# A Mamba-2 scan without a state between its two chunks, and five weight units whose low halves are made by ScalarE and a DMA

## The chip, the cores and the metric

The kernel runs on one core of a Trainium2 chip. The metric is device time in microseconds (us), the median of several executions. TensorE (PE) multiplies, VectorE (DVE), ScalarE (ACT) and GpSimd (POOL) do elementwise work, SyncE (SP) issues the loads of the weights, and POOL issues the other DMAs. Each engine runs its instructions in the order written, and waits on semaphores for the others.

## The reference

Two decoder layers over 256 tokens of width 1024, all in float32. Each layer is a half SwiGLU, a mixer and a half SwiGLU, each followed by a layer norm. The mixer of the first layer is sparse attention; the mixer of the second, which matters here, is a Mamba-2 scan in two chunks of 128 tokens, 32 heads of 64 in 4 groups, state size 128:

```python
cb = jnp.einsum('bclgn,bcsgn->bcgls', cm, bm)
y_diag = jnp.einsum('bcgrls,bcsgrp->bclgrp', cb[:, :, :, None] * decay, xdt)
decay_to_end = jnp.exp(a_cs_l[:, :, -1:] - a_cs_l)
states = jnp.einsum('bclgn,bclgrp->bcgrpn', bm, xdt * decay_to_end[..., None])
...
y_off = jnp.einsum('bclgn,bcgrpn->bclgrp', cm, prev) * jnp.exp(a_cs_l)[..., None]
return (y_diag + y_off).reshape(bsz, seq, n_h, p_dim)
```

The state is zero before the first chunk, so `prev` of the second chunk is `states` of the first, and `y_off` matters for the second chunk alone.

## The kernel before

**Weights.** All weights are streamed from HBM as 512 KB tiles `raw` (128 partitions by 1024). A "unit" is one such tile, split for TensorE into a high half `wh` (ACT, rounded to fp32r, line 327; line 325 where a scale is folded in) and a low half `wl` = raw - wh (DVE, lines 352 and 349). Each product is three matmuls: high by high, high by low, low by high (`mm3`, lines 530 to 532). The class `Weights` plans this: `make` emits a high half and puts the unit on the list `late`, `lows` emits the low halves of that list, `prefetch` (called there) issues the next loads on SP, `pump` calls these as units are used up. At most 10 split units exist (`SLOTS`); in the scan layer 4 raw tiles are in flight (`W.raws = 4`). In the SwiGLU layers some sums of weight tiles are made by accumulating DMAs from POOL's queue (`add`, line 267). Raw tiles share the 12 buffers "f4" with other 128x1024 tiles.

**The scan layer** (`ssd`) has 58 units, called u to u+57 here. Its order is written out by hand: units 0 to 9 for the gate z and dt, 10 to 17 for B and C (`bc_tile`), 18 to 21 for x of group 0, and then for each group g a list `f` of eight pieces of projection work, between which the steps of the scan are put. In groups 0 and 1 these are the x tiles of the next group (units 22 to 25 and 30 to 33, banks `pxs`) and the z columns (26 to 29 and 34 to 37); in group 2 the last x tiles (38, 40, 42, 44) and the first units of the output matrix (39, 41, ...), which alone carry a scale (line 325). Units are split some ten units ahead of their use. For group g the scan does, in this order:

```python
f[0](); x_tok(0, g); x_tok(1, g); x_end(g); f[1](); f[2]()
py[0] = diag(0, g); state(g); gate(0, g, py[0]); decay_load(0, g + 1); f[3]()
carry(g); square(0); root(0); py[1] = diag(1, g); gate(1, g, py[1]); decay_load(1, g + 1); f[4](); ...
```

`diag` is 8 products in plain float32 (two passes each, so 16 matmuls, L1534), into one of the two PSUM banks `ptr`; `gate` (DVE, L1551 and L1552) reads that bank; `decay_load` is a DMA on POOL's queue (L1436, tile `M`, an f4 buffer). `state` multiplies B with x (L1540) and copies the result to SBUF (ACT, L1542); `carry` multiplies C with that (L1546) and adds it to chunk 1 (DVE, L1547 and L1548). B in token order (`btok`) comes from four transposes (`b_tr`, L1470, and ACT's copy L1471), beside the products of C and B of each chunk (`cb`, L1477).

Of the kernel before, what the change touches and what calls it, by code (L numbers as in the profile page):

```python
# [10 lines left out]
F32 = mybir.dt.float32  # L11
F32R = mybir.dt.float32r
AF = mybir.ActivationFunctionType
ALU = mybir.AluOpType
# [10 lines left out]
KVR = 256  # L25
# [7 lines left out]
RMS_EPS = 1e-6  # L33
# [8 lines left out]
class Plan:  # L42
# [5 lines left out]
    def __init__(self):  # L48
        self.raws, self.forms = [], []
# [159 lines left out]
class Weights:  # L209

    def __init__(self, nc, raw_tile, split_pool, src, widths, forms, slots, raws):
        self.nc, self.raw_tile, self.sp, self.src = nc, raw_tile, split_pool, src
        self.widths, self.forms, self.slots, self.raws = widths, forms, slots, raws
        self.offs = np.concatenate([[0], np.cumsum(np.array(widths) * 128)]).tolist()
        self.n, self.nraw = len(forms), len(widths)
        self.loaded = self.summed = self.made = self.done = self.dead = self.debt = 0
        self.defer = False  # L220
        self.scale = {}
        self.raw, self.hl, self.late = {}, {}, []
        self.uses = {}
        self.added, self.prior = set(), {}
        self.adds = [u for u, f in enumerate(forms) if f[2]]
        last = {}
        for u, f in enumerate(forms):
            self.prior[u] = last.get(f[0], (-1, None))
            last[f[0]] = (u, u)
            if f[1] is not None:  # L230
                last[f[1]] = (last.get(f[1], (-1, None))[0], u)
            for r in f[:2]:
                if r is not None:
                    self.uses[r] = self.uses.get(r, 0) + 1
# [75 lines left out]
    def make(self, between=None):  # L310

        nc, u = self.nc, self.made
        r = self.forms[u][0]
        if self.summed <= u:
            self.sum()
        raw = self.raw[r]
        w = self.widths[r]  # L320
        h = self.sp.tile([128, 1024], F32R, name=f"wh{u}", tag="wh", bufs=self.slots)
        lo = self.sp.tile([128, 1024], F32R, name=f"wl{u}", tag="wl", bufs=self.slots)
        for c, n in self.parts(u):
            if u in self.scale:
                nc.scalar.activation(h[:, c:c + n], raw[:, c:c + n], AF.Copy, scale=self.scale[u])
            else:
                nc.scalar.copy(h[:, c:c + n], raw[:, c:c + n])  # L327
            if between:
                nc.vector.tensor_sub(lo[:, c:c + n], raw[:, c:c + n], h[:, c:c + n].bitcast(F32))
                if not c:  # L330
                    between()
        if between:
            self.used(r)
        else:
            self.late.append(u)
        self.hl[u] = (h, lo)
        self.made += 1
        self.owe(w)
# [70 lines left out]
def trunk_kernel(ctx: ExitStack, tc: tile.TileContext, widths, forms, x, ln_g, ln_b, wts, kvg, convp,  # L409
                 dt_bias, a_log, d_skip, norm_g, out):  # L410
    nc = tc.nc
# [17 lines left out]
    def f2(s):  # L429
        return wk.tile([128, 512], F32, name=nm(s), tag="f2", bufs=9)  # L430
# [26 lines left out]
    def ptr():  # L457
        return psum.tile([128, 512], F32, name=nm("ptr"), tag="ptr", bufs=2)
# [54 lines left out]
    dsk = consts.tile([128, SH], F32, name="dsk")  # L513
    nc.gpsimd.dma_start(dsk, bcast_rows(d_skip, 0, SH))

    def rsqrt_pool(src, eps):

        n = src.shape[1]
        e = tiny("rse")
        nc.gpsimd.tensor_scalar(e[:, :n], src, float(eps), None, op0=ALU.add)  # L520
        o = tiny("rs")
        nc.gpsimd.tensor_tensor(o[:, :n], e[:, :n], mhalf.to_broadcast([128, n]) if n > 1 else mhalf, op=ALU.pow)
        return o[:, :n]
# [445 lines left out]
    def attention(xT, u, ln_i):  # L969
# [13 lines left out]
            nc.scalar.activation(sq, lt[t][:, :KVR], AF.Square, accum_out=ss[t][:, 0:1])  # L983

        def latent_norm(t):
            nc.vector.tensor_scalar(ss[t][:, 1:2], ss[t][:, 0:1], 1.0 / KVR, None, op0=ALU.mult)
            rc = rsqrt_pool(ss[t][:, 1:2], RMS_EPS)
            ki[t] = f1("ki")
            nc.vector.tensor_copy(ki[t][:, :128].rearrange("p (a d) -> p a d", a=2),
                                  lt[t][:, KVR + IH:NA_ATTN][:, None, :].to_broadcast([128, 2, HD]))  # L990
            wi = lt[t][:, KVR:KVR + IH]
            nc.vector.tensor_scalar(wi, wi, IH ** -0.5, None, op0=ALU.mult)
            nc.vector.tensor_scalar(lt[t][:, :KVR], lt[t][:, :KVR], rc, None, op0=ALU.mult)
# [336 lines left out]
    def ssd(xT, u, ln_i):  # L1330
# [57 lines left out]
        first_out = u + 10 + 8 + 4 + 16 + 1  # L1388
        for k in range(16):
            W.scale[first_out + (2 * k if k < 4 else 3 + k)] = ng_sb[:, k:k + 1]  # L1390
        spare[0] = 0

        def z0(t, c):
# [68 lines left out]
            W.pump(1 + i % 2)  # L1462

        cbm = f4("cbm")
        btok = f2("btok")

        def b_tr():
            pt = pspare(4)
            for g in range(SG):
                nc.tensor.transpose(pt[:, g * 128:(g + 1) * 128], bT[:, g * 256:g * 256 + 128], ident)  # L1470
            nc.scalar.copy(btok, pt)  # L1471

        def cb(t):
            pt = pspare(4)
            for g in range(SG):
                c = slice(g * 256 + t * 128, g * 256 + (t + 1) * 128)
                nc.tensor.matmul(pt[:, g * 128:(g + 1) * 128], bT[:, c], cTt[:, c], start=True, stop=True)  # L1477
            nc.vector.tensor_mul(cbm[:, t * 512:(t + 1) * 512].rearrange("p (g l) -> p g l", g=SG),
                                 pt.rearrange("p (g l) -> p g l", g=SG),
                                 tri[:, None, :].to_broadcast([128, SG, 128]))  # L1480
# [26 lines left out]
                                 .to_broadcast([128, 8, 128]))  # L1507

        yT = {}
        y, xd, xe, st, ss = {}, {}, {}, {}, {}  # L1510

        def x_tok(t, g):

# [21 lines left out]
                                 y[t][:, h * 64:(h + 1) * 64], start=True, stop=True)  # L1535
            return py

        def state(g):
            pst = ptr()
            nc.tensor.matmul(pst, btok[:, g * 128:(g + 1) * 128], xe[g], start=True, stop=True)  # L1540
            st[g] = f2("st")
            nc.scalar.copy(st[g], pst)  # L1542

        def carry(g):
            po = ptr()
            nc.tensor.matmul(po, cTt[:, g * 256 + 128:g * 256 + 256], st[g], start=True, stop=True)  # L1546
            nc.vector.tensor_mul(hv(xe[g]), hv(po), hb(eacs, g))  # L1547
            nc.vector.tensor_add(xd[1], xd[1], xe[g])  # L1548

        def gate(t, g, py):  # L1550
            nc.vector.tensor_add(y[t], py, xd[t])  # L1551
            nc.vector.tensor_mul(y[t], y[t], zs[g][:, t * 512:(t + 1) * 512])  # L1552
# [3 lines left out]
            nc.scalar.activation(xd[t], y[t], AF.Square, accum_out=ss[t][:, 0:1])  # L1556

        def root(t):
            nc.vector.tensor_scalar(ss[t][:, 1:2], ss[t][:, 0:1], 1.0 / 512, None, op0=ALU.mult)
            ss[t] = rsqrt_pool(ss[t][:, 1:2], RMS_EPS)  # L1560

        def norm(t):
            nc.scalar.activation(y[t], y[t], AF.Copy, scale=ss[t])
# [55 lines left out]
        for i in range(4):  # L1619
            xs_tile(0, i, u + i)  # L1620
            if i == 0:
                b_tr()
                cb(0)
                cb(1)
        decay_seg(0, 0)
        z_half(1, 1, 1, uz)
        flush()
# [8 lines left out]
        for g in range(SG):  # L1636
# [17 lines left out]
            f[1]()  # L1654
            f[2]()
            py[0] = diag(0, g)
            state(g)
            gate(0, g, py[0])
            if g < 3:
                decay_load(0, g + 1)  # L1660
            f[3]()
            carry(g)
            square(0)
            root(0)
            py[1] = diag(1, g)
# [80 lines left out]
```

## Time and profile before

| | |
|---|---|
| median of 3 runs | 1033.83 us (1033.52 to 1034.04) |
| profiled execution, own time | 1036.27 us |
| its span (first to last instruction) | 1034.6 us, 1.67 us less than its own time |
| busy in the span | PE 98%, DVE 85%, ACT 62%, POOL 10% |
| mean granted clock of TensorE | 0.997 of full speed |
| chain that ended last | PE 77%, DVE 11%, DMA 5%, issue 3%, ACT 2%, POOL 1% |

A busy share of PE counts a matmul from its start to its modelled end; matmuls overlap, so how full PE is shows in the distance between the starts of successive matmuls. The scan layer lies between about 640 and 840 us of the span.

### The profile page before, as it was taken

How to read it: one execution, taken by the hardware profiler on the slowest of the kernel's cores; microseconds unless marked ns; L12 is line 12 of the kernel's file. 1: busy time of each engine (PE TensorE's matmuls, PEld its weight loads, DVE VectorE, ACT ScalarE, POOL GpSimd, SP SyncE). 2: the span in 40 equal slices, each digit the busy share in tenths (PEclk: the TensorE clock that was granted, in tenths of full speed). 3: DMA queues.
4: the chain of work that ended last, by engine and by line, in shares of the span. 5: the costliest groups of instructions: out<-in, count | busy, mean ns of one | idle time of the engine just before them, and what ended most of it. 6: DMA issues, size and time to landing. Idle time of an engine off the chain costs nothing.

```text
span 1034.6 us, 14878 instructions
## 1 busy us (share of the span) xinstructions
PE 1016.9 (98%) x5427; PEld 862.3 (83%) x5427; DVE 876.3 (85%) x1299; ACT 637.9 (62%) x977; POOL 100.0 (10%) x158
## 2 busy tenths in 40 slices
PE   9999999999999999999999999999999999999986
PEld 7888888898788888888888888999888888888775
DVE  6889987788899789878978987699999889798784
ACT  6667675476656666744666774586776536656650
POOL 2011000100000011000000100240011110101001
PEclk9999999999999999999999999999999999999999
DMA  9768998352657777974687795455556657679741
GB/s 334 281 153 285 270 339 286 92 173 82 203 183 226 215 192 253 334 268 155 211 240 191 246 332 218 162 159 170 191 178 201 229 178 244 135 223 280 224 157 41
DMA packets 61641, 220.70 MB, mean 213 GB/s; under 512 B 6944, under 2 KB 7008, under 8 KB 61568
## 3 DMA queue, kind: packets, MB, share of 16 engines
q1 hardware_dynamic: 51264, 183.43, 50.0%
q0 software_dynamic: 10016, 35.81, 16.8%
q8 instruction: 42, 0.69, 0.3%
q10 hardware_dynamic: 288, 0.52, 0.1%
q14 instruction: 31, 0.25, 0.1%
HBM read 193.48 MB, written 1.08 MB: 188 GB/s over the span
## 4 chain that ended last, share of the span: by engine, by line
PE 77%; DVE 11%; DMA 5%; issue 3%; ACT 2%; POOL 1%; SPq 0%; POOLq 0%; DVEq 0%; ACTq 0%
PE pmm L532 9%; PE pmm L530 8%; PE pmm L531 8%; PE acc L530 8%; PE acc L531 8%; PE acc L532 8%; DVE wl L352 6%; DMA raw<-raw 4%; PE ptr L679 4%; PE pmm L679 4%; PE ptr L681 2%; PE pmm L681 2%; PE pxs L530 1%; PE pxs L532 1%; PE pxs L531 1%
## 5 line engine op out<-in xcount | busy, mean ns | idle before, releaser
L352 DVE TENSOR_TENSOR wl<-raw,wh 128x1024 fp32r<-128x1024 f32 (+2 forms) x404 | 475.5, 1214 | 14.8 <-ACT wh L327 14.4
L327 ACT CAST wh<-raw 128x1024 fp32r<-128x1024 f32 (+2 forms) x406 | 407.8, 1044 | 112.3 <-DVE raw L294 46.6
L530 PE MATMUL acc<-wh,hH 128*128 128x512 f32 (+1 forms) x352 | 137.6, 391 | 0.0
L532 PE MATMUL acc<-wh,hL 128*128 128x512 f32 (+1 forms) x352 | 136.6, 388 | 0.0
L531 PE MATMUL acc<-wl,hH 128*128 128x512 f32 (+1 forms) x352 | 136.5, 388 | 0.0
L530 PE MATMUL pmm<-wh,xT 128*128 128x512 f32 (+2 forms) x288 | 114.5, 397 | 0.8 <-ACT c L944 0.8
L532 PE MATMUL pmm<-wh,xT 128*128 128x512 f32 (+2 forms) x288 | 111.2, 386 | 0.2 <-DVE xT L527 0.2
L531 PE MATMUL pmm<-wl,xT 128*128 128x512 f32 (+2 forms) x288 | 110.8, 385 | 0.1
L267 POOL DMA_DIRECT2D raw<-raw x48 | 41.7, 869 | 439.8 <-DVE raw L294 149.2
L532 PEld LDWEIGHTS acc<-wh,hL 128*128 128x128 f32 x352 | 66.1, 188 | 13.8
L530 PEld LDWEIGHTS acc<-wh,hH 128*128 128x128 f32 x352 | 66.2, 188 | 12.8
L531 PEld LDWEIGHTS acc<-wl,hH 128*128 128x128 f32 x352 | 66.2, 188 | 12.6
L532 PE MATMUL pmm<-wh,xf 128*128 128x512 f32 x192 | 74.7, 389 | 0.0
L530 PE MATMUL pmm<-wh,xf 128*128 128x512 f32 x192 | 74.7, 389 | 0.0
L531 PE MATMUL pmm<-wl,xf 128*128 128x512 f32 x192 | 74.7, 389 | 0.0
L532 PEld LDWEIGHTS pmm<-wh,xT 128*128 128x128 f32 x288 | 54.1, 188 | 12.3 <-DVE xT L527 1.5
L531 PEld LDWEIGHTS pmm<-wl,xT 128*128 128x128 f32 x288 | 54.4, 189 | 10.5 <-DVE wl L352 1.3
L530 PEld LDWEIGHTS pmm<-wh,xT 128*128 128x128 f32 x288 | 54.3, 188 | 10.0 <-ACT c L944 1.0
L294 DVE TENSOR_TENSOR raw<-raw,raw 128x1024 f32<-128x1024 f32 x48 | 58.0, 1222 | 0.4
L679 PE MATMUL pmm<-xT,wh 128*128 128x512 f32 x192 | 50.8, 408 | 0.0
L679 PE MATMUL ptr<-xT,wh 128*128 128x512 f32 x192 | 47.9, 392 | 0.0
L530 PE MATMUL pxs<-xT,wh 128*128 128x256 f32 x160 | 46.4, 290 | 0.0
(313 smaller groups left out, 1899.7 us busy)
## 6 DMA issues: line engine op xcount, KB each, us to landing
raw<-in_wts_dram SPq DMA_DIRECT2D x339, 512.0 KB, 5.2
raw<-raw POOLq DMA_DIRECT2D x48, 512.0 KB, 6.0
M<-scr POOLq DMA_DIRECT2D x8, 512.0 KB, 5.2
lng<-in_ln_g_dram POOLq DMA_DIRECT2D x6, 512.0 KB, 5.6
lnb<-in_ln_b_dram POOLq DMA_DIRECT2D x6, 512.0 KB, 6.2
raw<-in_wts_dram SPq DMA_DIRECT2D x4, 408.0 KB, 5.0
out_dram<-x SPq DMA_DIRECT2D x4, 256.0 KB, 2.1
raw<-in_wts_dram SPq DMA_DIRECT2D x2, 492.0 KB, 4.8
```

The source lines that it names most:

```text
L267: self.nc.gpsimd.dma_start(self.raw[r], self.raw[other], accum_op=ALU.add)
L294: self.nc.vector.tensor_add(self.raw[r], self.raw[r], self.raw[other])
L327: nc.scalar.copy(h[:, c:c + n], raw[:, c:c + n])
L352: self.nc.vector.tensor_sub(lo[:, s], raw[:, s], h[:, s].bitcast(F32))
L530: nc.tensor.matmul(ps, lh, rh, start=first, stop=False, skip_group_check=on)
L531: nc.tensor.matmul(ps, lh, rl, start=False, stop=False, skip_group_check=on)
L532: nc.tensor.matmul(ps, ll, rh, start=False, stop=last, skip_group_check=on)
L679: nc.tensor.matmul(ps, H[:, k * 128:(k + 1) * 128], xT.HL[:, k, :], start=k == 0, stop=False)
L681: nc.tensor.matmul(ps[:, :SEQ], L[:, k * 128:(k + 1) * 128], xT.H[:, k, :], start=False, stop=k == DK - 1)
```

## The change

Three edits. (1) `b_tr` and `state` are gone. In their place `cb_cross` multiplies B of chunk 0 with C of chunk 1 once for each group, into a tile `cross`; `carry` multiplies `cross` with x directly, and stands where `state` stood, ahead of `f[3]`. (2) For the units 22, 26, 30, 34 and 38 of the scan layer the low half is not made by DVE: ACT writes -round(raw) into it (a copy with scale -1), and a DMA on POOL's queue adds raw to it. The raw tile counts as used at once. (3) `rsqrt_pool` multiplies by a scale itself, so that ten tiny DVE multiplications (two in the attention layer, L986, eight in the scan layer, L1559) go; the twelve layer norms use the same two-step form with scale 1.

```diff
+        self.by_dma = set()
...
+        if u in self.by_dma:
+            nc.scalar.activation(lo, raw, AF.Copy, scale=-1.0)
+            nc.gpsimd.dma_start(lo.bitcast(F32), raw, accum_op=ALU.add)
+        if between or u in self.by_dma:
             self.used(r)
         else:
             self.late.append(u)
...
-        nc.gpsimd.tensor_scalar(e[:, :n], src, float(eps), None, op0=ALU.add)
+        nc.gpsimd.tensor_scalar(e[:, :n], src, float(scale), float(eps), op0=ALU.mult, op1=ALU.add)
...
-            nc.vector.tensor_scalar(ss[t][:, 1:2], ss[t][:, 0:1], 1.0 / KVR, None, op0=ALU.mult)
-            rc = rsqrt_pool(ss[t][:, 1:2], RMS_EPS)
+            rc = rsqrt_pool(ss[t][:, 0:1], RMS_EPS, 1.0 / KVR)
...
+        W.by_dma = set(u + i for i in (22, 26, 30, 34, 38))
...
-        def b_tr():
+        def cb_cross():
             pt = pspare(4)
             for g in range(SG):
-                nc.tensor.transpose(pt[:, g * 128:(g + 1) * 128], bT[:, g * 256:g * 256 + 128], ident)
-            nc.scalar.copy(btok, pt)
+                c = slice(g * 256 + 128, g * 256 + 256)
+                nc.tensor.matmul(pt[:, g * 128:(g + 1) * 128], bT[:, g * 256:g * 256 + 128], cTt[:, c],
+                                 start=True, stop=True)
+            nc.scalar.copy(cross, pt)
...
-        def state(g):
-            pst = ptr()
-            nc.tensor.matmul(pst, btok[:, g * 128:(g + 1) * 128], xe[g], start=True, stop=True)
-            st[g] = f2("st")
-            nc.scalar.copy(st[g], pst)
-
         def carry(g):
             po = ptr()
-            nc.tensor.matmul(po, cTt[:, g * 256 + 128:g * 256 + 256], st[g], start=True, stop=True)
+            nc.tensor.matmul(po, cross[:, g * 128:(g + 1) * 128], xe[g], start=True, stop=True)
...
-            nc.vector.tensor_scalar(ss[t][:, 1:2], ss[t][:, 0:1], 1.0 / 512, None, op0=ALU.mult)
-            ss[t] = rsqrt_pool(ss[t][:, 1:2], RMS_EPS)
+            ss[t] = rsqrt_pool(ss[t][:, 0:1], RMS_EPS, 1.0 / 512)
...
             if i == 0:
-                b_tr()
                 cb(0)
                 cb(1)
+                cb_cross()
...
             py[0] = diag(0, g)
-            state(g)
             gate(0, g, py[0])
+            carry(g)
             if g < 3:
                 decay_load(0, g + 1)
             f[3]()
-            carry(g)
             square(0)
             root(0)
```

## Rows read from the trace of the kernel before

**Rows 1.** The page, part 1 (busy us, share of the span, instructions) and the first line of part 4 (the chain that ended last, shares of the span by engine).

```profile
PE 1016.9 (98%) x5427; PEld 862.3 (83%) x5427; DVE 876.3 (85%) x1299; ACT 637.9 (62%) x977; POOL 100.0 (10%) x158
PE 77%; DVE 11%; DMA 5%; issue 3%; ACT 2%; POOL 1%; SPq 0%; POOLq 0%; DVEq 0%; ACTq 0%
```

**Rows 2.** Busy time by stretch in the scan layer: stretch, its length, busy us and instructions (x) of PE, PEld, DVE, ACT, POOL, then the granted clock of TensorE, the DMA engines' busy share and GB/s.

```profile
714.00:735.00 21.00, 20.19 (x141) 17.92 (x141) 20.13 (x38) 11.70 (x19) 1.95 (x4) 1.00 0.30 103
735.00:760.00 25.00, 25.00 (x176) 22.44 (x175) 23.87 (x46) 19.54 (x29) 1.46 (x4) 1.00 0.58 190
760.00:790.00 30.00, 30.00 (x189) 26.22 (x189) 28.35 (x52) 20.95 (x32) 2.87 (x6) 1.00 0.54 176
```

**Rows 3.** The timeline in group 0 of the scan, from `state` to the second `diag`: start us, us, engine, line, operation; in brackets idle time before it and what ended it. The last two rows are matmuls of 512 columns of a z piece.

```profile
723.15 1.08 PE L1540 MATMUL ptr<-xe,btok 128*128 128x512 f32 x2
723.67 0.68 PE L530 MATMUL pxs<-xT,wh 128*128 128x256 f32 x1
...
724.18 0.28 PE L531 MATMUL pxs<-xT,wh 128*128 128x256 f32 x1
...
724.28 1.22 DVE L352 TENSOR_TENSOR wl<-raw,wh 128x1024 fp32r<-128x1024 f32 x1
724.30 0.28 PE L532 MATMUL pxs<-xT,wl 128*128 128x256 f32 x1
...
726.94 1.02 PE L1546 MATMUL ptr<-st,cTt 128*128 128x512 f32 x2
...
727.97 0.69 DVE L1551 TENSOR_TENSOR xdt<-ptr,xtok 128x512 f32<-128x512 f32 x1
...
728.71 2.00 PE L1534 MATMUL ptr<-xdt,M 128*128 128x64 f32 x16 [0.75 <-DVE xdt L1551]
...
731.07 0.40 PE L532 MATMUL pmm<-wh,xT 128*128 128x512 f32 x1
...
731.30 0.40 PE L530 MATMUL pmm<-wh,xT 128*128 128x512 f32 x1
```

**Rows 4.** The same place in group 1: the gate on DVE, `carry` and the second `diag` on PE.

```profile
757.65 0.68 DVE L1551 TENSOR_TENSOR xdt<-ptr,xtok 128x512 f32<-128x512 f32 x1
757.67 1.02 PE L1546 MATMUL ptr<-st,cTt 128*128 128x512 f32 x2
...
758.53 0.44 PE L1534 MATMUL ptr<-xdt,M 128*128 128x64 f32 x3
```

**Rows 5.** PE's timeline at `b_tr` (L1470) and `cb` (L1477), and the first matmul behind them.

```profile
697.02 0.60 PE L1470 MATMUL psp<-ident,bT 128*128 128x128 f32 x4
697.46 2.07 PE L1477 MATMUL pmm<-cTt,bT 128*128 128x128 f32 x16
699.28 0.36 PE L530 MATMUL pxs<-xT,wh 128*128 128x256 f32 x1
```

**Rows 6.** Groups of instructions between 690 and 840 us: line, engine, operation, tiles, count | busy us, mean ns of one | idle before them.

```profile
L352 DVE TENSOR_TENSOR wl<-raw,wh 128x1024 fp32r<-128x1024 f32 x26 | 31.5, 1218 | 0.3 <-ACT wh L327 0.3
L327 ACT CAST wh<-raw 128x1024 fp32r<-128x1024 f32 x25 | 25.9, 1039 | 5.5 <-PE acc L532 5.5
...
L325 ACT ACTIVATE wh<-raw,ng_sb 128x1024 fp32r<-128x1024 f32 x16 | 17.9, 1140 | 0.0
...
L1542 ACT COPY st<-ptr 128x512 f32<-128x512 f32 x4 | 2.3, 582 | 7.7 <-PE ptr L1540 7.7
...
L1559 DVE TENSOR_SCALAR ss<-ss 128x1 f32<-128x1 f32 x8 | 1.2, 148 | 0.0
```

**Rows 7.** The accumulating DMAs that the kernel already has (line 267, all in the SwiGLU layers): their issue on POOL (duration ns min/median/max), and their time from issue to landing.

```profile
L267 POOL DMA_DIRECT2D raw<-raw x48: 852/862/954, 52.3 to 967.5; - x48
...
DMA to landing us min/median/max: 4.5/6.0/11.9
```

**Rows 8.** ACT's timeline: the high half of unit 30 of the scan layer, that of unit 38, and that of unit 39, the first with a scale. Between the first two lie seven more rows of L327, one for each of the units 31 to 37.

```profile
718.42 1.04 ACT L327 CAST wh<-raw 128x1024 fp32r<-128x1024 f32 x1
...
747.23 1.05 ACT L327 CAST wh<-raw 128x1024 fp32r<-128x1024 f32 x1
...
750.25 1.14 ACT L325 ACTIVATE wh<-raw,ng_sb 128x1024 fp32r<-128x1024 f32 x1
```

**Rows 9.** PE's timeline: the first matmul that uses unit 30 (the first x tile of group 2).

```profile
742.66 0.28 PE L530 MATMUL pxs<-xT,wh 128*128 128x256 f32 x1
```

**Rows 10.** POOL's timeline: loads of M whose issue waited in POOL's queue for a buffer.

```profile
723.84 0.53 POOL L1436 DMA_DIRECT2D M<-scr  x1 [24.97 <-DVE cv L1452]
...
754.35 0.62 POOL L1436 DMA_DIRECT2D M<-scr  x1 [17.34 <-PE ptr L1534]
```

**Rows 11.** The last SwiGLU layer: its last accumulating DMA in POOL's timeline, and PE's timeline around the longest gap of PE behind it.

```profile
967.51 0.89 POOL L267 DMA_DIRECT2D raw<-raw  x1 [0.84 <-issue]
...
990.95 0.38 PE L763 MATMUL ptr<-ident,c 128*128 128x128 f32 x2
...
994.13 0.63 PE L763 MATMUL ptr<-ident,h 128*128 128x128 f32 x2 [2.80 <-DVE hL L768]
994.41 3.59 PE L679 MATMUL pmm<-xT,wh 128*128 128x512 f32 x8
```

**Rows 12.** Busy time by stretch behind that gap (columns as in rows 2).

```profile
994.00:996.00 2.00, 1.87 (x6) 1.58 (x7) 2.00 (x4) 1.20 (x2) 0.00 (x0) 0.56 0.48 190
```

**Rows 13.** The last layer norm, the end of the kernel: DVE's scaling behind POOL's root.

```profile
1029.68 1.42 DVE L637 SCALAR_TENSOR_TENSOR x<-x,rs,lnb 128x512 f32<-128x512 f32 x2 [0.46 <-POOL rs L522]
```

More of the change, by code (lines that the diff above doesn't have):

```diff
@@ L331, in make @@
                     between()
-        if between:
+        if u in self.by_dma:
+            nc.scalar.activation(lo, raw, AF.Copy, scale=-1.0)
+            nc.gpsimd.dma_start(lo.bitcast(F32), raw, accum_op=ALU.add)
+        if between or u in self.by_dma:
             self.used(r)
@@ L514, in trunk_kernel, with rsqrt_pool @@
     nc.gpsimd.dma_start(dsk, bcast_rows(d_skip, 0, SH))
-    def rsqrt_pool(src, eps):
+    def rsqrt_pool(src, eps, scale=1.0):
         n = src.shape[1]
         e = tiny("rse")
-        nc.gpsimd.tensor_scalar(e[:, :n], src, float(eps), None, op0=ALU.add)
+        nc.gpsimd.tensor_scalar(e[:, :n], src, float(scale), float(eps), op0=ALU.mult, op1=ALU.add)
         o = tiny("rs")
@@ L1464, in ssd @@
         cbm = f4("cbm")
-        btok = f2("btok")
-        def b_tr():
+        cross = f2("cross")
+        def cb_cross():
             pt = pspare(4)
             for g in range(SG):
-                nc.tensor.transpose(pt[:, g * 128:(g + 1) * 128], bT[:, g * 256:g * 256 + 128], ident)
-            nc.scalar.copy(btok, pt)
+                c = slice(g * 256 + 128, g * 256 + 256)
+                nc.tensor.matmul(pt[:, g * 128:(g + 1) * 128], bT[:, g * 256:g * 256 + 128], cTt[:, c],
+                                 start=True, stop=True)
+            nc.scalar.copy(cross, pt)
         def cb(t):
@@ L1509, in ssd @@
         yT = {}
-        y, xd, xe, st, ss = {}, {}, {}, {}, {}
+        y, xd, xe, ss = {}, {}, {}, {}
         def x_tok(t, g):
```

## The prediction

> **What bounds the kernel now.** I read the page first. PE is busy 98% of the span and carries 77% of the chain that ended last, DVE 85% and 11%, ACT 62% and 2% [rows 1]. PE's share counts overlapping matmuls, so the next view is the timeline, where the reader is to look at the starts: matmuls of 256 columns follow each other every 0.12 us (724.18, 724.30), those of 512 columns every 0.23 us (731.07, 731.30), each while the one before is still running [rows 3]. A matmul that leaves the program shortens PE's stream by such a distance, not by its duration. Third, the stretches of the scan layer: DVE is busy 20.13 of 21 us, 23.87 of 25 and 28.35 of 30, hardly less than PE, with ACT at 11.70, 19.54 and 20.95 [rows 2]. Two engines are nearly full, so the question is which waits for which. In group 0 PE waits: the second `diag` starts at 728.71 after 0.75 us without a matmul, released by the gate on DVE [rows 3]. In group 1 it doesn't, but only just: the gate starts at 757.65, the `diag` at 758.53 [rows 4]. From gate start to `diag` start group 0 takes 0.74 us, so in group 1 it could have started at 758.39, and 0.14 us is to spare. PE sets the pace, and DVE follows with almost no reserve.
>
> The profiled execution took 1036.27 us with a span of 1034.6; the runs have a median of 1033.83, 2.44 us less. I work out differences in the profiled span and take them from the median. What a measurement of this kernel can tell from no change is about 0.2%, 2.07 us.
>
> **The product instead of the state.** From the start of `state` to the second matmul behind it are 1.03 us (723.15 to 724.18); without `state` that would be one step of 0.12, so it costs PE 0.91 us [rows 3], and four groups 3.64 us. `carry` keeps its two matmuls; they only stand earlier, where `state` stood, and need the same `xe`. The four transposes of `b_tr` take 0.44 us of PE's stream (697.02 to 697.46), the sixteen matmuls of `cb` 1.82 (697.46 to 699.28) [rows 5]. `cb_cross` has eight of these: 0.91 us, 0.47 more than `b_tr`. PE's stream thus gets shorter by 3.64 - 0.47 = 3.17 us. Bounds: 2.7 if a lone fp32 product costs twice the extra that I give it, 3.6 if `cross` hides in a wait. ACT loses four copies of 0.58 us [rows 6], which nothing waits for once `state` is gone; the copy of `cross` takes the place of that of `btok`.
>
> `carry`'s DVE work (L1547, L1548) now stands right behind the gate, ahead of the convolutions of `f[3]`, which wait some 1.4 us longer. Behind these wait the release of a `pxs` bank, of which there are three, and the next x tile; both have a whole piece of PE work as cover. One bound: if the second `diag` got the bank that `carry` used, it would also wait for L1552 and L1547, two operations of some 0.7 us like the gate's 0.69 [rows 3], which in group 0 costs about 1.4 us. I take none of it, since in group 0 `carry` ran at 726.94, ahead of the gate at 727.97 [rows 3]: it took the bank that had been given up first, not the one that the gate still had to read.
>
> **Five low halves.** DVE loses 5 x 1.218 = 6.09 us [rows 6]. ACT gains five copies; the nearest rows are 1.039 us (L327) and 1.140 (L325) [rows 6], so 5.2 to 5.7 us; in the 76 us of rows 2 it is busy 52.2 [rows 2], so there is room, and I take 1.04 each. POOL gains five issues of 0.86 us and five transfers, which land 6.0 us after issue in the middle, 11.9 at worst [rows 7]. PE must not need the low half before. Unit 38 is the last high half ahead of the first scaled one (750.25), and seven lie between it and unit 30, so unit 30 is split at 718.42 [rows 8] and used first at 742.66 [rows 9], 24.2 us later. One more copy, the issue and the landing make 1.04 + 0.86 + 6.0 = 7.9 us, at worst 13.8. The transfers are hidden; without that cover each late microsecond would stop PE for one. The raw buffer comes free with the DMA's landing instead of DVE's subtraction (724.28 to 725.50 for unit 30 [rows 3]), some 2 us later, and SP's next loads with it; the same 24 us of lead cover that. Behind the DMA in POOL's queue stand the loads of M and the roots, which wait for ACT's copy, a microsecond, for nothing else.
>
> What DVE's relief is worth is read at the gates. In group 0 one of the two low halves ahead of the gate is unit 30's (724.28) [rows 3]. Units 22 and 26 lie earlier, where DVE still has gaps, and help nothing here. The gate comes 1.22 us sooner, less about 0.1 because ACT's extra copy holds up the convolution before it: at 726.85, with the bank free at 727.59. PE's own stream, with 0.86 us for `carry` (757.67 to 758.53 [rows 4]), would have come to that `diag` at 727.80, a stall of 0.91; now it comes 0.91 - 0.47 = 0.44 sooner, at 727.36. The stall falls to 0.23 us: 0.68 saved (bounds 0 and 0.91). In group 1 PE comes 0.44 + 0.68 + 0.91 = 2.03 us sooner, with 0.14 to spare before; the gate comes 3 x 1.22 = 3.66 sooner (units 30, 34 and 38 lie before it). No stall; the reserve carries through groups 2 and 3, where PE gains 0.91 each.
>
> **The roots.** The eight small multiplications are 8 x 0.148 = 1.2 us of DVE [rows 6], hidden behind PE; the two in the attention layer likewise. The layer norms' POOL step has two operations now. The one place without cover is the end, where DVE waits 0.46 us for POOL [rows 13]; I take no change there, and bound it by +-0.46.
>
> **Sum.** -3.17 - 0.68 = -3.85 us, all ahead of 840 us. The tail and the last SwiGLU layer are released by PE's sums and move with it. 1033.83 - 3.85 = 1030.0; the profiled span would be 1030.8. The likeliest case reaches from 1028.9 (3.6 + 0.91 + 0.46 gained) to 1031.2 (2.7 gained and the stall as it was); what is worse than that is a rival.
>
> **Rivals.**
> (a) DVE sets the scan's pace throughout. For it: the stretches at 95 to 96% [rows 2]. Then the gain is DVE's loss, 6.09 + 1.2 = 7.3 us: 1026.5. Against it: between the waits PE's matmuls follow at 0.12 and 0.23 us [rows 3], and a stream only 3.17 us shorter can gain no more than that and the stalls. The Trainium skill (Perfetto Trace Analysis, Identifying the Most-Contended Engine) says that PE's busy share misleads and that the share of weight loads is to be read instead. That share is 83% here, under DVE's 85%, and by that rule DVE would be the bound and 1026.5 the time; the distances between starts speak against it, as they show no room that the weight loads leave.
> (b) The last SwiGLU layer changes. Its last accumulating DMA, issued at 967.51, is followed by a gap of PE from 990.95 to 994.13, some 3.0 us beyond the two transposes [rows 11]. Behind it the granted clock is 0.56 of full speed [rows 12], close to the lower level of 1.2 GHz, and eight matmuls of 512 columns take 3.59 us [rows 11], where starts 0.23 us apart and a last one of 0.40 would make 2.0 [rows 3]. Together 4.6 us that hang on the order of transfers. If the shift undoes it: 1025.4; if the same happens once more: 1034.6. Nothing in the change touches it but the shift and the rotation of buffers, and all loads there follow PE's progress.
> (c) Slower: a low half lands late. POOL's queue is in order, and loads of M stood 24.97 and 17.34 us idle in it [rows 10]. Unit 30 can wait 24.2 - 7.9 = 16.3 us; behind the longer of these waits it would be 8.7 us late: 1038.7. It decides from about 20 us of waiting on, where the gain is used up. Against it: unit 30's split, at 718.42, is written ahead of the load issued at 723.84. The Trainium skill (SBUF — State Buffer, section "SBUF: two separate sides") says that POOL can't write descriptors while DVE holds the port they share in its faster copy modes. The issues here took 852 to 954 ns beside a DVE busy 85% [rows 7], so no run here shows such a block.
> (d) The gain is half eaten: by ACT's added copies ahead of convolutions and `x_tok`, or by the other bank in group 0. 1031.2 to 1033.8.
>
> **Chances.** Forecast 0.64; (a) 0.08; (b) undone 0.06, once more 0.06; (c) 0.05; (d) 0.11. The range 1026.5 to 1033.0 leaves out (b) on both sides, (c) and the upper part of (d), 0.2 in all. Faster than 1031.76: forecast, (a), (b) undone and a fifth of (d), 0.80; within 0.2%: (b) once more and most of (d), 0.14; slower: (c) and a rest, 0.06.
>
> **What would show it.** In the trace after: `carry` right behind the first `diag`, no matmul of `state`; the second `diag` of group 0 with a wait of 0.2 to 0.3 us, later ones without; DVE some 7 us less busy in the scan layer, with gaps where it had none; the five new DMAs landing 6 us after issue and never named as what PE waited for; the layer norm's end about 4 us earlier at 840; the gap at 991 of the same size, 4 us earlier. The prediction is wrong if PE waits at a new place between 700 and 820, or if the 4 us are there at 840 and gone at the end.

## The result and the profile after

The changed kernel takes 1029.09 us (median of 6 runs, 1027.81 to 1030.28), the kernel before 1034.09 beside it (6 runs); the ratio is 0.9946, 95% interval 0.9932 to 0.9959, or 5.6 us less (5.0 by the two medians). The profiled execution took 1028.57 us with a span of 1026.9, against 1036.27 and 1034.6 before.

The page after, part 1 and the first line of part 4 (columns as in [rows 1]):

```profile
PE 1012.5 (99%) x5423; PEld 861.4 (84%) x5423; DVE 869.6 (85%) x1284; ACT 640.4 (62%) x978; POOL 107.7 (10%) x163
PE 81%; DVE 9%; DMA 4%; issue 2%; ACT 2%; POOL 1%; POOLq 0%; DVEq 0%; ACTq 0%
```

DVE is busy 6.7 us less, PE's part of the chain has grown from 77% to 81%. The stretches of the scan layer (columns as in [rows 2]) show DVE hardly emptier, which fits PE bringing it the same work sooner:

```profile
714.00:735.00 21.00, 20.46 (x148) 18.83 (x147) 20.16 (x38) 14.35 (x21) 3.69 (x6) 1.00 0.52 147
735.00:760.00 25.00, 25.00 (x179) 23.00 (x178) 22.50 (x45) 19.93 (x31) 2.51 (x4) 1.00 0.80 231
760.00:790.00 30.00, 30.00 (x190) 26.59 (x189) 28.46 (x50) 21.15 (x30) 5.18 (x9) 1.00 0.56 188
```

Group 0 of the scan in the timeline after, to be held against [rows 3]: the first `diag`, `carry` right behind it, the gate on DVE, and the second `diag`:

```profile
722.34 1.97 PE L1542 MATMUL ptr<-xdt,M 128*128 128x64 f32 x16
...
724.15 1.08 PE L1549 MATMUL ptr<-xe,cross 128*128 128x512 f32 x2
...
727.83 0.68 DVE L1554 TENSOR_TENSOR xdt<-ptr,xtok 128x512 f32<-128x512 f32 x1
...
728.57 2.00 PE L1542 MATMUL ptr<-xdt,M 128*128 128x64 f32 x16 [0.48 <-DVE xdt L1554]
```

The second `diag` still waits, 0.48 us instead of 0.75. And there is a wait that was not there before, in the first of the products that follow the C tiles (timeline after, to be held against [rows 5]):

```profile
697.11 0.83 PE L1485 MATMUL psp<-cTt,bT 128*128 128x128 f32 x6
...
697.78 0.41 ACT L1449 ACTIVATE cTt<-cv 128x256 f32<-128x256 f32 x1
...
698.23 0.49 PE L1485 MATMUL psp<-cTt,bT 128*128 128x128 f32 x2 [0.29 <-ACT cTt L1449]
...
700.26 0.36 PE L535 MATMUL pxs<-xT,wh 128*128 128x256 f32 x1
```

The 0.29 us are idle time; by the starts the wait is some 0.4 us, since six such matmuls at the 0.11 us of [rows 5] would put the seventh at 697.8 and not at 698.23.

Where the time went is best read from the start of the same matmul in two traces. Each kernel was profiled twice (the second time in the experiments below):

```
start, us                        before   again   | after    again
first matmul of the x tiles      669.55   669.17  | 669.64   670.19
first one behind cb and cross    699.28   698.90  | 700.26   700.82
second diag, group 0             728.71   728.33  | 728.57   729.12
second diag, group 1             758.53   758.16  | 757.36   757.92
second diag, group 2             788.09   787.70  | 785.96   786.50
second diag, group 3             817.33   816.93  | 814.33   814.90
transposes after the pause       994.13   992.15  | 988.05   988.50
end of the span                 1034.6   1031.0   |1026.9   1027.3
```

From the first line to group 3 the change gains 3.1 us in either pair (147.78 and 147.76 before, 144.69 and 144.71 after). From there to the transposes it gains another 3.1 (first pair) or 1.6 (second). All of it lies late in the last SwiGLU layer, where the change touches nothing: from group 3 to the matmul that starts at 976.38 in before (973.35 after) the four profiles take 159.02 to 159.05 us, and from there to the transposes 17.75, 16.18, 14.70 and 14.56 (in the first profile of before PE also waits 0.75 us at 982 for ACT's copy behind the same landing). Behind the transposes the four take 40.47, 38.85, 38.85 and 38.80: the first profile of before lost 1.6 us more to the granted clock of 0.56 [rows 12].

The last SwiGLU layer after, to be held against [rows 11]: its last two accumulating DMAs on POOL, ACT's next cast behind their landing, and the transposes on PE (timeline):

```profile
962.45 1.75 POOL L269 DMA_DIRECT2D raw<-raw  x2 [10.30 <-DVE wl L357]
...
973.45 2.00 ACT L329 CAST wh<-raw 128x1024 fp32r<-128x1024 f32 x2 [3.45 <-DMA raw<-raw]
...
988.05 0.44 PE L768 MATMUL ptr<-ident,h 128*128 128x128 f32 x2 [1.06 <-DVE hL L773]
```

The stretch behind them (columns as in [rows 2]):

```profile
988.00:990.00 2.00, 1.95 (x10) 1.64 (x11) 2.00 (x4) 1.47 (x3) 0.00 (x0) 1.00 0.54 203
```

The pause of 2.80 us is 1.06 now, and the clock stays at 1.00. One more thing differs: before, the last accumulating DMA was issued 1.71 us after the one ahead of it (965.80 to 967.51), 0.84 of them idle with "issue" as the reason, that is, with nothing that the profile shows to wait for [rows 11]. Now both stand in one row of 1.75 us, 0.90 apart. The row of before ahead of the one in [rows 11]:

```profile
965.80 0.87 POOL L267 DMA_DIRECT2D raw<-raw  x1 [9.95 <-DVE wl L352]
```

### The profile page after: what moved, and what is told of

The parts are those of the page before. It is cut to its first block, busy times and chain, and to the rows that moved or that the text cites. A ratio compares the mean times of both kernels' runs of the same rounds, so it can differ in the third digit from the quotient of the medians.

```text
span 1026.9 us, 14872 instructions
## 1 busy us (share of the span) xinstructions
PE 1012.5 (99%) x5423; PEld 861.4 (84%) x5423; DVE 869.6 (85%) x1284; ACT 640.4 (62%) x978; POOL 107.7 (10%) x163
## 4 chain that ended last, share of the span: by engine, by line
PE 81%; DVE 9%; DMA 4%; issue 2%; ACT 2%; POOL 1%; POOLq 0%; DVEq 0%; ACTq 0%
PE pmm L537 9%; PE pmm L535 9%; PE pmm L536 9%; PE acc L535 8%; PE acc L537 8%; PE acc L536 8%; DVE wl L357 5%; PE ptr L684 4%; PE pmm L684 4%; DMA raw<-raw 4%; PE ptr L686 2%; PE pmm L686 2%; PE pxs L535 2%; PE pxs L537 1%; PE pxs L536 1%
## 5 line engine op out<-in xcount | busy, mean ns | idle before, releaser
L357 DVE TENSOR_TENSOR wl<-raw,wh 128x1024 fp32r<-128x1024 f32 (+2 forms) x399 | 469.1, 1212 | 15.6 <-ACT wh L329 15.1
```

What stands on the lines that cost most here:

```text
L357: self.nc.vector.tensor_sub(lo[:, s], raw[:, s], h[:, s].bitcast(F32))
```

## The experiments

Theory A (the prediction): the gain is PE's shorter stream plus a shorter stall in group 0, all in the scan layer, and needs both halves of the change. Theory B: a good part comes from the last SwiGLU layer, where something other than the arithmetic changed.

### The two halves apart

Without the five DMAs (the changed kernel, all low halves back on DVE), and the five DMAs alone (the kernel before, with `by_dma` and nothing else):

```diff
-        W.by_dma = set(u + i for i in (22, 26, 30, 34, 38))
+        W.by_dma = set()
```

```diff
+        self.by_dma = set()
...
-        if between:
+        if u in self.by_dma:
+            nc.scalar.activation(lo, raw, AF.Copy, scale=-1.0)
+            nc.gpsimd.dma_start(lo.bitcast(F32), raw, accum_op=ALU.add)
+        if between or u in self.by_dma:
...
+        W.by_dma = set(u + i for i in (22, 26, 30, 34, 38))
```

> The changed kernel with the set of DMA-made low halves empty: DVE makes all low halves again. PE theory with DVE at the gates (mine, as the trace of after mends it): PE's stream is 3.0 us shorter, but the gates come no sooner. Second diag of group 0: stall 0.91 + 0.86 = about 1.8 us; group 1 had 0.14 us to spare and now stalls some 0.7; groups 2 and 3 stall little. PE at 820 us stands 0.5 to 1.5 us ahead of before instead of 3.2; time 0.5 to 1.5 us under before if the last SwiGLU layer is as in before. Rival, PE alone sets the pace and the DMA-made low halves are idle ornament: 3 us ahead at 820, no stall above 0.9. Rival, DVE sets the pace throughout: at 820 within 0.3 us of before.

> The kernel before with only the five low halves by negated copy and DMA (state, b_tr and the roots as before). PE theory: PE's stream is unchanged, only the wait of 0.91 us at the second diag of group 0 falls away: PE 0.8 to 1.1 us ahead of before at 820. Rival, DVE sets the pace: 6 us ahead. Rival, the low halves land late or ACT's extra copies hold PE up: not ahead, a new wait of PE between 690 and 820.

Beside them the two kernels themselves ran once more:

> The kernel before, unchanged, profiled once more, for the gap of PE near 991 us in the last SwiGLU layer (3.0 us, and 1.6 us at a low granted clock behind it). If the gap hangs on chance within an execution (POOL issued the last accumulating DMA 0.84 us late without a wait), it differs here by a microsecond or more. If it belongs to the program, it is again 2.5 to 3.5 us with the low clock behind it. PE at 820 us within 0.3 us of the first profile either way.

> The changed kernel, unchanged, profiled and timed once more. If the missing gap in the last SwiGLU layer belongs to the change, it is missing again (under 0.5 us). If it is chance, a gap of 1 to 3 us may show. PE at 820 us 3.0 to 3.4 us ahead of before in both cases. Time 4 to 7 us under before.

Measured: without the DMAs 1034.44 us, ratio 0.9999 (0.9982 to 1.0017); the DMAs alone 1031.13, ratio 0.9964 (0.9952 to 0.9976); the changed kernel again 1028.49, ratio 0.9946 (0.9930 to 0.9962). In the second profiles the pause of the last SwiGLU layer is 2.54 us before, with the clock at 1.00 behind it, and 0.92 after, where under 0.5 had been expected. So the long pause goes with the program, and the low clock behind it does not.

Without the DMAs, the gate and the second `diag` of group 0 (timeline), and the granted clock behind it (stretches, columns as in [rows 2]):

```profile
729.62 0.68 DVE L1554 TENSOR_TENSOR xdt<-ptr,xtok 128x512 f32<-128x512 f32 x1
...
730.36 0.95 PE L1542 MATMUL ptr<-xdt,M 128*128 128x64 f32 x5 [1.62 <-DVE xdt L1554]
```

```profile
729.00:731.00 2.00, 0.64 (x5) 0.64 (x5) 1.97 (x4) 1.58 (x3) 0.00 (x0) 0.95 0.16 39
731.00:737.00 6.00, 6.00 (x22) 5.23 (x22) 5.86 (x10) 2.38 (x6) 1.71 (x3) 0.50 0.58 203
```

PE comes sooner and waits for the same DVE work: 1.62 us, and 0.68 at the second `diag` of group 1 (some 1.8 and 0.7 were expected). In this execution the granted clock then falls to 0.50, the 1.2 GHz level, for some 6 us, which costs 3.2 us more (PE's starts are 1.64 us behind those of before at the start of that `diag`, and 4.87 at the matmuls that before starts from 735 on). By group 3 this kernel has lost 2.2 us in the scan layer; without the low clock it would, by this estimate, have won 1.0, within the 0.5 to 1.5 expected. So without relief for DVE the stalls take most of the shorter stream; theory A holds there, and the price of a miss was larger than the stall alone. The time of the whole kernel does not show the 2.2 us: one profile shows one execution, and the mean clocks of this kernel's runs go from 0.992 to 0.999.

With the DMAs alone, at the same place:

```profile
729.06 0.68 DVE L1556 TENSOR_TENSOR xdt<-ptr,xtok 128x512 f32<-128x512 f32 x1
...
730.01 1.22 PE L1539 MATMUL ptr<-xdt,M 128*128 128x64 f32 x10
```

No wait of PE is left; the scan layer is 1.2 us shorter (669.55 to 817.33 before, 671.75 to 818.30 here: 146.55 instead of 147.78; 0.8 to 1.1 us were expected). But the time falls by 3.7. Some 2.5 us come from elsewhere, as 2.5 of the 5.6 do in the whole change. That is theory B.

### What sets the pause in the last SwiGLU layer

In the second profile of before, POOL, ACT and PE around it (timeline), and the stretch behind (columns as in [rows 2]):

```profile
967.25 0.89 POOL L267 DMA_DIRECT2D raw<-raw  x1 [0.84 <-issue]
...
977.54 2.00 ACT L327 CAST wh<-raw 128x1024 fp32r<-128x1024 f32 x2 [3.47 <-DMA raw<-raw]
...
992.15 0.44 PE L763 MATMUL ptr<-ident,h 128*128 128x128 f32 x2 [2.54 <-DVE hL L768]
```

```profile
992.00:994.00 2.00, 1.85 (x9) 1.59 (x10) 2.00 (x4) 1.38 (x3) 0.00 (x0) 1.00 0.61 236
```

And in the first, ACT's cast and DVE's work ahead of PE's release:

```profile
979.52 1.99 ACT L327 CAST wh<-raw 128x1024 fp32r<-128x1024 f32 x2 [6.02 <-DMA raw<-raw]
...
990.25 3.49 DVE L352 TENSOR_TENSOR wl<-raw,wh 128x1024 fp32r<-128x1024 f32 x3
993.66 0.42 DVE L768 TENSOR_TENSOR hL<-ptr,hH 128x256 fp32r<-128x256 f32 x1
```

The chain: the last accumulating DMA lands; ACT, which is in order, casts that sum only then; all its later casts and DVE's low halves follow back to back; three low halves (3.49 us) stand ahead of the small hL on DVE for which PE waits. From that cast to PE's transposes it is 14.61 us in the first profile of before (979.52 to 994.13), 14.61 in the second (977.54 to 992.15), 14.60 after (973.45 to 988.05). It is 14.60 or 14.61 in all fourteen profiles of this study. So the landing sets the pause. Why was the issue late? First guess: the place of that DMA in POOL's sequence of instructions. The kernel before with eight instructions more on POOL:

```diff
+    pad = consts.tile([128, 1], F32, name="pad")
+    for _ in range(8):
+        nc.gpsimd.memset(pad, 0.0)
```

> The kernel before with eight tiny memsets on POOL at its start, written to a tile that nothing reads; nothing else is changed. In both profiles of before, and in that of the changed kernel without the DMA-made low halves, POOL issues the last accumulating DMA 0.84 us late without a wait, at the same place of its instruction stream (the 290th or so); where five DMAs more stand in POOL's stream, it does not. Theory that the place in POOL's stream makes the delay: here it has moved off the last accumulating DMA, which is issued 0.9 us behind the one before (1.7 in before); it lands 1 us or so sooner and the gap of PE near 991 shrinks from 2.7 to 3.0 us to 1.2 to 2.0; time 1 to 3 us under before, with the scan layer unchanged. Rival, the delay comes from the buffers or the order of loads that the DMA-made low halves change: nothing changes here, the gap stays at 2.5 to 3.1 us.

Measured: 1035.15 us, ratio 1.0010 (0.9997 to 1.0023). The same DMA is late by the same time:

```profile
968.31 0.89 POOL L267 DMA_DIRECT2D raw<-raw  x1 [0.84 <-issue]
```

The guess falls. In the kernel before, with the eight fills or without, and in the changed one without its DMAs, that transfer is the 73rd of the 75 that POOL issues. In the kernels with five more it is the 78th, and is not late. So the next kernels add nothing but tiny transfers: one, or five, at the start, beside the other constants.

```diff
+    pad = consts.tile([128, 5], F32, name="pad")
+    for i in range(5):
+        nc.gpsimd.dma_start(pad[:, i:i + 1], bcast_rows(d_skip, i, 1))
```

> As the kernel with five more transfers, but with one more. By the count, the late one is then the accumulating transfer just ahead of the last (965.80 in before), at which POOL waits 9.95 us for DVE anyway: the lateness is hidden in that wait, and the last is issued 0.90 us after it, with a pause of 1.9 to 2.4 us. If the count doesn't matter, the last one is still issued 1.71 us after the one ahead of it and the pause is 2.8 to 3.1 us.

> The kernel before with five tiny transfers more on POOL's queue, issued with the other constants at the start of the kernel (one column of d_skip each, into a tile that nothing reads); everything else is as before. In before, the 73rd of POOL's 75 transfers is the last accumulating one of the last SwiGLU layer, and it is issued 0.84 us late with nothing to wait for. Theory 'the late issue belongs to the 73rd transfer of the queue': it moves to what was the 68th, the last accumulating transfer is issued 0.90 us after the one ahead of it instead of 1.71, lands about 0.8 us sooner, the pause of PE that follows it shrinks from 2.8-3.1 to 1.9-2.4 us, and the time falls by 0.8 to 2 us (ratio 0.998 to 0.9992). Theory 'it belongs to this transfer or this layer': still 1.71 us, pause 2.8 to 3.1, ratio 1.000.

With one more (POOL and PE):

```profile
966.88 1.80 POOL L267 DMA_DIRECT2D raw<-raw  x2 [10.75 <-DVE wl L352]
...
993.30 0.44 PE L766 MATMUL ptr<-ident,h 128*128 128x128 f32 x2 [2.81 <-DVE hL L771]
```

The last one now stands in one row with the one ahead of it (1.80 us for both), as the count says; but that one, now the 73rd, is issued after 10.75 us of idling where it was 9.95: it is late by 0.80, and was not hidden in its wait as I had expected. Both then land as late as before, and the pause stays (1033.86 us, one run). With five more:

```profile
968.40 1.77 POOL L267 DMA_DIRECT2D raw<-raw  x2 [9.94 <-DVE wl L352]
...
978.73 2.00 ACT L327 CAST wh<-raw 128x1024 fp32r<-128x1024 f32 x2 [3.15 <-DMA raw<-raw]
...
993.34 0.44 PE L766 MATMUL ptr<-ident,h 128*128 128x128 f32 x2 [0.77 <-DVE hL L771]
```

Neither is late, and the pause is 0.77 us. Yet the time is 1034.43, ratio 1.0005 (0.9997 to 1.0014): PE reached the x tiles at 672.08 instead of 669.17 to 669.55. In its first 22 us it had waited 0.43 and 0.76 us for low halves, which it does not in before; how the tiny transfers bring that about was not followed. To have the one without the other, the five were moved to where POOL is idle, behind a pair of LayerNorm loads:

```diff
+    pad = consts.tile([128, 5], F32, name="pad")
...
+        if i == 1:
+            for k in range(5):
+                nc.gpsimd.dma_start(pad[:, k:k + 1], bcast_rows(d_skip, k, 1))
```

> The kernel before with the same five tiny transfers more on POOL's queue, now issued behind the second layer's loads of the LayerNorm rows, near 162 us, where POOL has nothing to do for 16 us, instead of at the start, where they delayed the constants and cost PE some 2 us. Theory 'the count of transfers decides where the late issue falls, and it costs time where it hits the last accumulating transfer': the start is as in before, the last accumulating transfer is issued 0.90 us after the one ahead, PE's pause in the last SwiGLU layer is 1.0 to 1.9 us instead of 2.8 to 3.1, and the time is 1 to 2 us less (ratio 0.998 to 0.999). Theory 'the shorter pause is given back elsewhere, as the whole gain was in the first form of this kernel': ratio 0.9995 or more.

They turned out to be issued at 264 us, not near 162. POOL, ACT and PE:

```profile
264.15 2.76 POOL L604 DMA_DIRECT2D pad<-in_d_skip_dram  x5
...
965.93 1.77 POOL L267 DMA_DIRECT2D raw<-raw  x2 [10.36 <-DVE wl L352]
...
976.19 2.00 ACT L327 CAST wh<-raw 128x1024 fp32r<-128x1024 f32 x2 [2.68 <-DMA raw<-raw]
...
990.80 0.44 PE L767 MATMUL ptr<-ident,h 128*128 128x128 f32 x2 [0.30 <-DVE hL L772]
```

Measured: 1031.71 us, ratio 0.9965 (0.9951 to 0.9979), 3.6 us less, more than the 1 to 2 expected. Five transfers that carry nothing anyone reads give the kernel before two thirds of the change's gain; its scan layer is as long as ever (670.09 to 817.86, 147.77 us). Theory B is shown.

The late issue has not gone from these kernels; it stands elsewhere. In the changed kernel it is still the 73rd transfer, an earlier accumulating one, that is late by 0.82 us. Its row, and below it that of the same transfer in the kernel without the five DMAs:

```profile
928.21 0.87 POOL L269 DMA_DIRECT2D raw<-raw  x1 [11.06 <-issue]
```

```profile
933.35 0.86 POOL L269 DMA_DIRECT2D raw<-raw  x1 [10.24 <-DVE wl L357]
```

With the five tiny ones it is not the 73rd but the 75th. It follows 1.37 us behind the end of the DVE sum (L294) that releases it, where the same transfer in before follows 0.54 behind (below it):

```profile
948.93 1.23 DVE L294 TENSOR_TENSOR raw<-raw,raw 128x1024 f32<-128x1024 f32 x1
...
951.53 0.90 POOL L267 DMA_DIRECT2D raw<-raw  x1 [15.85 <-ACT wh L327]
```

```profile
949.22 1.22 DVE L294 TENSOR_TENSOR raw<-raw,raw 128x1024 f32<-128x1024 f32 x1
...
950.98 0.87 POOL L267 DMA_DIRECT2D raw<-raw  x1 [15.76 <-DVE raw L294]
```

At both places PE shows no wait for it.

### What was left in the scan layer

Three edits of the changed kernel. `flush` ahead of the last z half, against waits of DVE's `x_tok`; `cb` and `cb_cross` behind the second x tile instead of the first, against the new wait for the last C tile; and the low half of unit 31 instead of those of 22 and 26:

```diff
-        z_half(1, 1, 1, uz)
         flush()
+        z_half(1, 1, 1, uz)
```

> The changed kernel with the last SiLU of the x tiles of group 0 (flush) written ahead of the z piece behind it, so that ACT does it while PE works on that piece. My theory: PE's wait of 0.82 us at the last transpose of x_tok (near 712 us), which both kernels have, falls away, and the rest of the scan follows: PE 0.8 us further ahead at 820, since DVE starts its part sooner by the same. Rival, DVE takes it back at the gate of group 0: the wait there grows from 0.64 to some 1.4 us and 0 to 0.2 us is won.

```diff
-            if i == 0:
+            if i == 1:
                 cb(0)
                 cb(1)
                 cb_cross()
```

> The changed kernel with cb(0), cb(1) and cb_cross one x tile later. In the changed kernel PE waits 0.45 us in cb(0) for ACT's SiLU of the last C tile; before, the four transposes of b_tr, which need only B, stood there as cover. My theory: the wait is gone here, PE 0.4 to 0.5 us further ahead at 820. Rival, the wait comes from elsewhere (the PSUM bank): it stays, 0 us.

```diff
-        W.by_dma = set(u + i for i in (22, 26, 30, 34, 38))
+        W.by_dma = set(u + i for i in (30, 31, 34, 38))
```

> The changed kernel with the DMA-made low halves of units 30, 31, 34 and 38 instead of 22, 26, 30, 34 and 38. My theory: only low halves that DVE makes between the first gates are worth anything. Without 22 and 26 nothing is lost; with 31, whose low half (1.2 us of DVE) stands right ahead of the gate of group 0, the gate comes some 1.1 us sooner and PE's wait of 0.64 us at the second diag of group 0 falls to 0 to 0.1: PE 0.6 us further ahead at 820. Rival, each of the five counts alike: 1 us of DVE less is relieved and PE is 0.2 to 1 us behind the changed kernel.

> The changed kernel with units 30, 31, 34 and 38 by transfers instead of 22, 26, 30, 34 and 38, now timed. Its one look had the wait at the second diagonal product of group 0 at 0.21 us instead of 0.64, and nothing worse. Theory 'units 22 and 26 bring nothing, and unit 31 eases DVE just ahead of that wait': 0.4 us below the changed kernel, ratio to before 0.9940 to 0.9945. Theory 'the relief of 22 and 26 is wanted somewhere': ratio 0.9946 or more.

The first took 1032.15 us (one run): the wait that it aimed at is gone, and the first `diag` of group 0 waits for M instead, with another wait in group 2. The scan layer is 146.26 us, 1.6 longer than in the changed kernel, where 0.8 less was expected:

```profile
723.46 0.74 PE L1542 MATMUL ptr<-xdt,M 128*128 128x64 f32 x5 [0.93 <-DVE M L1514]
...
782.34 0.47 PE L535 MATMUL acc<-wh,yH 128*128 128x512 f32 x1 [0.90 <-DVE xtok L1532]
```

The second took 1029.34 (one run): the wait for the last C tile is gone, and one of 0.38 us stands later. The scan layer is 144.72 us, so nothing is won:

```profile
780.11 0.47 PE L535 MATMUL acc<-wh,yH 128*128 128x512 f32 x1 [0.38 <-DVE xtok L1532]
```

The third had 1028.26 in its first run and 1028.85 over 5 runs, ratio 0.9949 (0.9936 to 0.9963). Its gate and second `diag` of group 0:

```profile
727.44 0.68 DVE L1554 TENSOR_TENSOR xdt<-ptr,xtok 128x512 f32<-128x512 f32 x1
...
728.18 2.00 PE L1542 MATMUL ptr<-xdt,M 128*128 128x64 f32 x16
```

Hardly a stall is left (0.2 us by the starts), and the scan layer is 144.29 us (669.68 to 813.97) instead of 144.7. The trace shows 0.4 us; the timing can't tell the kernel from the changed one. Units 22 and 26 bring nothing up to the first `diag` of group 0, as the prediction had it: from the first x matmul it is 52.70 us to there in both kernels. Behind it this run can't tell their loss from the gain of unit 31. No kernel tried was shown to beat the changed one.

## Why the prediction was right, and where it was not

The time came out 0.9 us below the forecast and inside the likeliest case's own range, but that is in part luck: the sum holds two errors of opposite sign. It put 3.85 us into the scan layer and nothing elsewhere; there were 3.1 in the scan layer, and about 2.5 in the last SwiGLU layer. (The upper end of that range, 1033.83 - 2.7, is 1031.1 and not 1031.2; nothing hangs on it.)

**The stream.** Right in size. In groups 1 and 3 the distance from the first to the second `diag`, which holds `state` before and not after, falls from 6.37 and 6.27 us to 5.51 and 5.41: 0.86 each, where 0.91 was taken.

**`cb_cross`.** Mis-sized. 0.47 us was its matmuls less the transposes; the stretch from the first x matmul to the one behind `cb` and `cross` grew by 0.89 (29.73 to 30.62). The rest is the new wait for ACT's last C tile (698.23): the four transposes of `b_tr` needed B alone and had covered it, which the prediction did not price. With `cb` one x tile later the wait was gone. It costed the edit by its own instructions and not by what the removed ones were covering.

**The stall in group 0.** The step that failed is "the stall falls to 0.23 us: 0.68 saved". Between the matmul behind `cb` and the second `diag` the change gains 1.12 us (29.43 to 28.31), of which 0.86 are `state`'s: 0.26 saved. The gate did come 1.12 us sooner, exactly as predicted, if counted from that same matmul (727.97 - 699.28 = 28.69, 727.83 - 700.26 = 27.57). The mistake was the point from which the two engines were counted. The prediction made PE later by `cb_cross` and left DVE's chain where it was, though that chain starts from PE's products and shifts with them. The two halves apart show it: counted from the first x matmul, the gate starts at 58.42 us before, 57.31 with the DMAs alone, 59.34 without them (with `cb_cross` ahead of it and no relief for DVE), and 58.19 in the changed kernel. With both shifted, the stall is 0.91 + 0.86 - 1.12 = 0.65, which is what the trace has (0.64 between the starts, beyond one distance of 0.12).

**Groups 1 to 3.** Right: no stall, 1.03, 0.96 and 0.87 us gained in turn (29.82 to 28.79, 29.56 to 28.60, 29.24 to 28.37). The gate of group 1, though, came 1.42 us sooner, counted from the first x matmul (88.10 to 86.68), and not 3.66: the time to spare grew from 0.14 to 0.30 us (757.36 - 756.32, less 0.74). It was enough, but not for the reason given.

**Five low halves.** Right: DVE lost 6.7 us, 7.3 predicted; the five transfers were never named as what PE waited for. Their line and its landing times:

```profile
L336 POOL DMA_DIRECT2D wl<-raw x5: 882/900/958, 688.2 to 749.3; - x5
...
DMA to landing us min/median/max: 4.8/5.6/9.0
```

The median is 5.6 us, 6.0 was taken; rival (c) did not come up. But the step counted their issues on POOL by their time alone (0.86 us each). What they did besides is to change which transfer is POOL's 73rd.

**The rivals.** (a), DVE as the pace: the scan layer gave 3.1 us and not 7.3, with DVE 6.7 us lighter; the five low halves off DVE alone gave 1.2. The Trainium skill's rule on the share of weight loads (Perfetto Trace Analysis, Identifying the Most-Contended Engine) would have picked DVE; the trace disagrees. (b), the gap of the last SwiGLU layer undone: it happened in part, 2.80 us to 1.06 and the low clock gone, and it had been given 6 in 100, because "nothing in the change touches it but the shift and the rotation of buffers". That sentence is wrong, and [rows 11] held the thread: the 0.84 us with "issue" as their reason. (d), a smaller gain in the scan layer, came by 0.75 us of the 3.85, but by the wait for the C tile and the stall and not by the other bank: the second `diag` of group 0 starts 0.74 us behind its gate, as before.

**The sign that was to show it.** "About 4 us earlier at 840, the gap the same size" was the right one to look for, and it failed on both counts: 3.1 us, and a smaller gap. The second `diag` of group 0 waits 0.48 us, where 0.2 to 0.3 was said. The new wait of PE, at 698, lies just ahead of the stretch from 700 to 820 in which one was to show the prediction wrong.

## What to carry to other kernels

When an edit removes work, ask what that work was covering: here four transposes hid a wait that then cost about as much (0.42 us) as the new products did beyond them (0.47). A stall between two engines is worked out from the distance of both from a common release; shift both, not one. And when a total comes out right, compare it by stretches: nearly half of this gain lay where the edit has no line, and a kernel that adds nothing but five idle transfers showed it.

## What the runs showed of the hardware

- One of the transfers that POOL issues is 0.80 to 0.84 us late, with nothing to wait for. It is the 73rd of the queue in twelve of the fourteen profiles, whichever transfer that is, and the 75th in the two kernels with five tiny ones more. Eight more memory fills on POOL did not move it. One tiny transfer moved it by one transfer, four and five accumulating ones by four and five, five tiny ones by three only. So it is not the number of transfers alone that counts; what does, and what POOL does in that time, no run here separates.
- The Trainium skill (DMA: Bandwidth & Descriptors, section "SWDGE vs HWDGE vs iDMA") says that transfers issued from GpSimd go through descriptor rings that its cores fill in software. A ring that fills up or wraps would fit a delay that goes by what has been issued so far; that it is this, no run here shows.
- A late issue of 0.84 us cost more than that. From issue to landing the late transfer took 10.2 to 11.9 us in four profiles, the same transfer 9.3 to 9.4 with five tiny ones more on the queue (9.4 to 10.6 in the kernels with low halves by DMA). PE's pause was 2.5 to 2.8 us in the kernel before (2.1 in the changed one without its DMAs), and 0.3 to 0.8 with the five tiny ones.
- The granted clock fell to 0.50, the 1.2 GHz level, behind a wait of 1.62 us in group 0, and to 0.56 behind one of 2.80 in the last SwiGLU layer, but stayed at 1.00 behind one of 2.54 at the same place in the second profile of before. It fell to 0.50 behind 2.52 us there in the kernel with eight fills, and stayed at 1.00 behind 2.81 in the one with one tiny transfer more (the stretch behind the pause in these two, columns as in [rows 2], eight fills first). So the length of the pause alone does not decide it; where the clock fell, it cost 3.2 us in group 0 and 1.6 in the last layer of before.

```profile
994.00:996.00 2.00, 2.00 (x7) 1.52 (x6) 2.00 (x3) 1.95 (x3) 0.00 (x0) 0.50 0.22 88
```

```profile
994.00:996.00 2.00, 2.00 (x12) 1.70 (x11) 2.00 (x3) 2.00 (x3) 0.00 (x0) 1.00 0.22 82
```
